# Fixing VectorE's order through the second attention branch of a decoder block, with its bias made in two halves

## The chip, the cores and the metric

The kernel runs on one core of a Trainium2 chip. The metric is the time of one execution on the device, in microseconds (us). The engines are named as in the profile: PE is TensorE (PEld its weight loads), DVE is VectorE, ACT is ScalarE, POOL is GpSimd, SP is SyncE, which issues most DMAs.

## The reference

One layer of a decoder: 256 tokens, width 1024, float32. Two attention branches of eight heads of 64 share one input projection, their outputs are merged by a sigmoid gate, and a gated feed-forward network of width 2816 follows. With 256 tokens the block-sparse first branch is plain causal attention. The second branch adds a "forgetting" bias to its scores, and this is where the change lies:

```python
def forgetting_attention(q, k, v, log_f):
    c = jnp.cumsum(log_f, axis=-1)
    ...
        s = jnp.einsum('bhcd,bhsd->bhcs', qi, k, ...) * scale
        s = s + ci[..., None] - c[:, :, None, :]
        s = jnp.where(pos[None, :] <= qp[:, None], s, NEG_INF)
        p = jax.nn.softmax(s, axis=-1).astype(v.dtype)
...
proj = jnp.einsum('bsd,de->bse', rms_norm(x, attn_norm_g[l]), w_in[l])
qa, ka, va, qb, kb, vb, f_logit, g_logit = jnp.split(proj, bounds, axis=-1)
o_a = moba_attention(qa, ka, va)          # after head norms and rope
o_b = forgetting_attention(qb, kb, vb, log_sigmoid(f_logit + b_forget))
merged = gates[:, :, 0] * (o_a @ w_branch_moba) + gates[:, :, 1] * (o_b @ w_branch_fox)
x = x + merged @ w_out
u, g = jnp.split(rms_norm(x, ffn_norm_g) @ w_ffn_up, 2, axis=-1)
x = x + (silu(causal_depthwise_conv(g)) * u) @ w_ffn_down
```

## The kernel before

Every float32 matrix product is made of three products of a reduced type: an operand is split into an upper part (`whi`, `xh`, `oh`) and a lower rest (`wlo`, `xl`, `ol`), and upper times upper, lower times upper and upper times lower are added in PSUM. Weights come from memory in chunks of 128 x 2048 (`raw`, three buffers). Each chunk is split in two halves, "units" of 1024 columns: ScalarE copies the upper part (line 141) and VectorE subtracts it from the raw weight for the lower part (line 142). There are six buffers of `whi` and of `wlo`. A raw buffer is free for the next chunk's DMA when both of its units are split. `use` asks for a unit and starts splits some five units ahead.

The order of the chunks, and so of TensorE's work, is written in the list `chunks`. In the part that matters it is: gate 2 (`wg`, 2), the scores of the second branch, the V projection of the second branch (`qkv`, 3, in chunks 0 and 1, that is four units), gates 3, 4 and 5 (two units each), the transposes of both branches' probabilities (line 540), gate 6, the products with V (line 562), gate 7, then the output side and the feed-forward part.

TensorE runs in the order of the program. For the other engines a scheduler at compile time orders each queue, by priority (a block under `soon()` goes ahead of its place in the program) and by when it takes an instruction to be ready. `after(i, j)` adds an edge that keeps instruction i behind j in this order. On one engine that is only an order and costs no instruction; once compiled, each engine works off its queue strictly in turn.

VectorE's work in this part:

- `gate` (line 603) reads a gate's PSUM bank, scales it and writes it into `gates`.
- `forget_bias` (lines 451 to 465) makes the bias of all eight heads, 128 x 3072: per block of 128 keys a subtraction of the query's cumulated value (`cc`) from the keys' values (`cB`, which lies in the upper half of `gates` and is broadcast over the partitions by a DMA from GpSimd's queue, line 443), and for two of the three blocks an addition of the causal mask. These are five instructions of 128 x 1024.
- `scores` puts the four pairs of heads into six PSUM banks with small matmuls and has VectorE fill the unused corners with zeros (ten fills, line 489).
- `softmax` (line 508) reads each pair's scores from PSUM in four instructions, adds the bias, keeps the row's extreme in `nm` and writes to SBUF. ScalarE then takes four exponentials per pair (line 512), with sums in `l`, and VectorE the reciprocals `r` (line 516).
- `scale` multiplies by `r`: for pairs 0 and 1 of the second branch on GpSimd (line 524), for pairs 2 and 3 on VectorE (line 528, four instructions a pair); the first branch is scaled by ScalarE (line 530).

PSUM has eight banks, given out in turn. The six of the second branch's scores, the two of the V projection and then the bank of gate 3 follow each other. Gate 3's bank is therefore the first of the score banks again: pair 0's scores of the first head and part of pair 1's lie in it, so it is free when those are read.

Of the kernel before, what the change touches and what calls it, by code (L numbers as in the profile page):

```python
# [12 lines left out]
ALU = mybir.AluOpType  # L13
# [4 lines left out]
P = 128  # L18
# [4 lines left out]
HD = 64  # L23
NH = 8
# [20 lines left out]
def decoder_block(ctx, tc, a, out):  # L45
    nc = tc.nc
# [50 lines left out]
    moved = []  # L97
    sent_last = []
    first_lo = []
    state = {"next": 0, "raw": None, "lag": 0, "hi": None, "lo": None}  # L100

    def after(i, j):
# [2 lines left out]
    def load(upto):  # L105
        while state["next"] <= min(upto, len(units) - 1):
            c, h = units[state["next"]]
            if c[0] == "head":
                k = c[1]
                if k < 2:  # L110
                    raw = gates[:, 4 * k:4 * k + 4].rearrange("p a b t -> p (a b t)")
                    for s0, s1 in ((0, HX + W4), (HX + W4, HEADW)):
                        loads[c] = nc.sync.dma_start(raw[:, s0:s1], a["head"][k][:, s0:s1])
                    x, g, raw = raw[:, 0:S], raw[:, S:S + 1], raw[:, HX:HEADW]
                    nc.gpsimd.tensor_copy(xT[:, k], x)
                else:
                    if k % 2 == 0:
                        state["raw"] = T([P, 2048], "raw", RB)
                    raw = state["raw"][:, k % 2 * 1024:(k % 2 + 1) * 1024]
                    x, g = xT[:, k], g1[:, k:k + 1]  # L120
                    nc.sync.dma_start(x, a["head"][k][:, 0:S])
                    loads[c] = nc.sync.dma_start(raw, a["head"][k][:, HX:HEADW])
                xlo = split_x(k, x, g)
                at, n = 44, 2 if k < 2 else 1
            else:
                at, n = 44 if c[0] == "qkv" else 0, 1
                if h == 0:
                    src = a[c[0]]
                    for j in c[1:]:
                        src = src[j]  # L130
                    state["raw"] = T([P, 2048], "raw", RB)
                    loads[c] = nc.sync.dma_start(state["raw"], src)
                    if c in (("qkv", 0, 1), ("wg", 2)):
                        after(loads[c], sent_last[c == ("wg", 2)])
                raw = state["raw"][:, h * 1024:(h + 1) * 1024]
            hi = T([P, 1088], "whi", HB, F32R)[:, at:at + 1024]
            lo = T([P, 1088], "wlo", HB, F32R)[:, at:at + 1024]
            w = 1024 // n
            for j in range(n):
                s = slice(j * w, (j + 1) * w)  # L140
                i = nc.scalar.activation(hi[:, s], raw[:, s], AF.Copy)  # L141
                d = nc.vector.tensor_tensor(lo[:, s], raw[:, s], hi[:, s].bitcast(F32), op=ALU.subtract)  # L142
                if (c, h) == (("qkv", 1, 1), 0):
                    after(i, rs_done[0])
                    after(d, rs_done[1])
                if (c, h) == (("qkv", 1, 0), 0):
                    first_lo.append(d)
                if (c, h) == (("qkv", 0, 1), 0):
                    after(i, moved[0])
                if (c, h) in ((("qkv", 2, 1), 1), (("wg", 0), 1)):  # L150
                    after(d, state["qn"])
                if (c, h) == (("wg", 1), 0):
                    after(i, state["exp"])
                if (c, h) == (("qkv", 0, 0), 0):
                    state["v_lo"] = d
                if (c, h) == (("wg", 1), 1):
                    state["turn"] = d
                if (c, h) == (("qkv", 3, 0), 1):
                    state["v1_lo"] = d
                if (c, h) == (("qkv", 3, 1), 0):  # L160
                    after(i, state["v_out"])
                if c[0] == "head" and j == 0:
                    after(d, xlo)
                for this, last in ((i, state["hi"]), (d, state["lo"])):
                    if last is not None:
                        after(this, last)
            if c[0] == "head":
                square_x(k, x, i)
            split[c, h] = (hi, lo)
            state["last"] = i, d  # L170
            state["next"] += 1
# [276 lines left out]
            step = 6 if i < 2 else 2  # L448
            nc.gpsimd.tensor_copy(cc[32 * i:32 * (i + 1)], turned[:, i:i + step + 1:step, 0:NH])

    def forget_bias(done):

        bias = fg["bias"] = T([P, 3072], "bias").rearrange("p (n c) -> p n c", n=NH)
        for j, (kb, t) in enumerate([(0, 0), (1, 1), (0, 1)]):
            dst = bias[:, :, j * P:(j + 1) * P]
            src = fg["cB"][:, :, kb * P:(kb + 1) * P]
            if kb:
                d4, src = (v.rearrange("p n (h c) -> p n h c", h=2) for v in (dst, src))
                i = nc.vector.tensor_tensor(d4, src[:, :, ::-1], cc[:, t, :, None, None].to_broadcast([P, NH, 2, HD]), op=ALU.subtract)
                after(i, done)  # L460
            else:
                i = nc.vector.tensor_tensor(dst, src, cc[:, t, :, None].to_broadcast([P, NH, P]), op=ALU.subtract)
                after(i, done)
            if j != 2:
                nc.vector.tensor_tensor(dst, dst, mask3[:, None, j * P:(j + 1) * P].to_broadcast([P, NH, P]), op=ALU.add)


    probs = {}
    homes = []
    last_exp = []  # L470

    def scores(br, read):
        sps = [banks() for _ in range(3)]
        at = [((0, 0), (0, P)), ((0, 3 * P), (1, 0)), ((2, 0), (1, S)), ((2, P), (2, S))]
        def piece(n, t, j):
            b, o = at[n][t]
            return sps[b][j][:, o:o + (t + 1) * P]
        for n, pair in enumerate(range(4)):
            for t in range(NT):
                for c, q in enumerate(QUARTERS[t]):  # L480
                    seen = slice(0, (q + 1) * HD) if t == 0 else slice((3 - q) * HD, S)
                    keys = slice(seen.start + (1 - t) * P, seen.stop + (1 - t) * P)
                    for j, r in enumerate(halves):
                        nc.tensor.matmul(piece(n, t, j)[halves[c], seen], qTs[br][r, pair, q * HD:(q + 1) * HD], kTs[br][r, pair, keys], start=True, stop=True)
        for b, c, o in ((0, 0, slice(64, 512, 384)), (0, 1, slice(128, 129, 1)), (1, 1, slice(0, 512, 256)), (2, 0, slice(64, 256, 128)), (2, 1, slice(256, 257, 1))):
            for j in range(2):
                starts = range(o.start, o.stop, o.step)
                u = sps[b][j][halves[c]].rearrange("p (g c) -> p g c", c=HD)[:, o.start // HD:starts[-1] // HD + 1:max(1, o.step // HD)]
                after(nc.vector.memset(u, 0.0), read)
        return [[[piece(n, t, j) for t in range(NT)] for j in range(2)] for n in range(4)]  # L490

    def softmax(br, pair, sps, done, exp_behind=None):
# [11 lines left out]
        for j in range(2):  # L504
            h = 2 * pair + j
            sp = sps[j]
            for i, c in enumerate((slice(0, 128), slice(128, 384))):
                first = nc.vector.tensor_tensor_reduce(s[:, j, c], sp[i], mask3[:, c] if br == 0 else fg["bias"][:, h, c],
                                               scale=1.0, scalar=3e38, op0=ALU.add, op1=ALU.min, accum_out=nm[:, j, i:i + 1])
                after(first, done)  # L510
            for i, c in enumerate((slice(0, 128), slice(128, 384))):
                last_exp[:] = [nc.scalar.activation(s[:, j, c], s[:, j, c], AF.Exp, scale=-1.0, bias=nm[:, j, i:i + 1], accum_out=l[:, j, i:i + 1])]  # L512
                if exp_behind is not None:
                    after(last_exp[0], exp_behind)
# [5 lines left out]
    def scale(br, pair, last=None):  # L520
        s, r = probs[br, pair]
        for i, c in enumerate((slice(0, 128), slice(128, 384))):
# [2 lines left out]
                continue  # L525
            for j in range(2):
                if br:
                    nc.vector.tensor_scalar_mul(s[:, j, c], s[:, j, c], r[:, j, i:i + 1])
                else:
                    after(nc.scalar.activation(s[:, j, c], s[:, j, c], AF.Copy, scale=r[:, j, i:i + 1]), last)  # L530
        probs[br, pair] = s
# [130 lines left out]
    project(2, pv, 1)  # L662
    finish_v(pv, 0, last_exp[0])
    read = gate(2)
    after(read, state["v1_lo"])
    with soon():
        forget_bias(state["last"][1])
    for pair in range(4):
        scale(0, pair, state["last"][0])
    with soon():  # L670
        for pair, sp in enumerate(scores(1, read)):
            softmax(1, pair, sp, read)
            scale(1, pair)
# [1 line left out]
    project(5, pv, 0)  # L675
    project(5, pv, 1)
    finish_v(pv, 1)
    gate(3)
    gate(4)
    gate(5, hold=True)  # L680
    with soon():
# [212 lines left out]
```

## Time and profile before

| | us |
|---|---|
| median of 3 runs (361.47 to 362.01) | 361.87 |
| the profiled execution | 361.6 |
| its span, first to last instruction | 359.8 |
| PE busy | 352.3 (98%) |
| DVE busy | 278.4 (77%) |
| ACT busy | 221.7 (62%) |
| POOL busy | 44.6 (12%) |

A row of the order in time gives the start in us from the span's start, the duration, engine, line and operation, the tile written and those read, and how many instructions are merged in the row; in brackets stands idle time before it and what ended that. A row of waits gives waiter, what it waited for, total us, times and the longest. A row of the stretches gives the stretch, its length, and for each engine (PE, PEld, DVE, ACT, POOL) busy time and instructions, then TensorE's granted clock, the DMA share and GB/s. Ends of matmuls are modelled, so starts are used.

### The profile page before, as it was taken

The page shows a single profiled execution, that of the slowest core. Times are in us where ns is not written, and L with a number is a line of the kernel's source. Part 1 is how long each engine was busy: PE and PEld are TensorE (multiplying, and loading weights), DVE is VectorE, ACT ScalarE, POOL GpSimd, SP SyncE. Part 2 cuts the span into 40 slices and gives each one's busy share as a digit, 9 for nine tenths or more (in the row PEclk, how much of TensorE's full clock was granted, in tenths as well). Part 3 has the DMA queues.
Part 4 walks back from the last instruction along what each step waited for, and adds up shares of the span by engine and source line. Part 5 has one row for each costly group of instructions (what it writes and reads, how often), then busy time and mean ns, then how long its engine had stood idle before and what let it go on. Part 6 is the DMA issues. An engine that isn't in the chain of part 4 may idle for free.

```text
span 359.8 us, 7495 instructions
## 1 busy us (share of the span) xinstructions
PE 352.3 (98%) x3053; PEld 335.1 (93%) x3053; DVE 278.4 (77%) x476; ACT 221.7 (62%) x378; POOL 44.6 (12%) x69
## 2 busy tenths in 40 slices
PE   9999999999889999999999999999999999999995
PEld 5888899898789999999999999999999999999995
DVE  5899999979997668975969777768676866768643
ACT  5859644799984996645877554555464555546420
POOL 3432724230230000000530000000000000000000
PEclk9999999999999999999999999999999999999999
DMA  7987376958047454565464564564564564554003
GB/s 272 402 321 254 119 227 200 351 198 304 13 165 298 145 210 134 219 233 197 157 213 169 205 233 148 203 229 147 211 222 154 210 219 148 220 196 156 3 0 118
DMA packets 13475, 70.39 MB, mean 196 GB/s; under 512 B 2200, under 2 KB 3360, under 8 KB 6016
## 3 DMA queue, kind: packets, MB, share of 16 engines
q1 hardware_dynamic: 12624, 67.93, 52.9%
q0 software_dynamic: 672, 1.98, 1.7%
q8 instruction: 24, 0.39, 0.4%
q14 instruction: 11, 0.09, 0.1%
q10 hardware_dynamic: 144, 0.00, 0.0%
HBM read 66.75 MB, written 1.06 MB: 188 GB/s over the span
## 4 chain that ended last, share of the span: by engine, by line
PE 90%; ACT 5%; DVE 4%; issue 1%; DVEq 0%
PE bank L593 14%; PE bank L595 14%; PE bank L594 14%; PE bank L317 9%; PE bank L303 6%; PE bank L807 6%; PE bank L806 6%; PE bank L808 6%; PE bank L732 2%; PE bank L706 2%; DVE wlo L142 2%; PE bank L731 2%; PE bank L730 2%; PE bank L705 2%; PE bank L704 2%; ACT s L512 2%
## 5 line engine op out<-in xcount | busy, mean ns | idle before, releaser
L142 DVE TENSOR_TENSOR wlo<-raw,whi 128x1024 fp32r<-128x1024 f32 x120 | 146.8, 1230 | 47.3 <-ACT whi L141 47.0
L141 ACT ACTIVATE whi<-raw 128x1024 fp32r<-128x1024 f32 x120 | 125.2, 1059 | 62.7 <-PE bank L594 37.1
L595 PE MATMUL bank<-oh,wlo 128*128 128x256 f32 x352 | 96.8, 275 | 0.0
L593 PE MATMUL bank<-oh,whi 128*128 128x256 f32 x352 | 96.8, 275 | 0.0
L594 PE MATMUL bank<-ol,whi 128*128 128x256 f32 x352 | 96.8, 275 | 0.0
L593 PEld LDWEIGHTS bank<-oh,whi 128*128 128x128 f32 x352 | 66.1, 188 | 0.0
L595 PEld LDWEIGHTS bank<-oh,wlo 128*128 128x128 f32 x352 | 66.1, 188 | 0.0
L594 PEld LDWEIGHTS bank<-ol,whi 128*128 128x128 f32 x352 | 66.1, 188 | 0.0
L593 PE MATMUL bank<-xh,whi 128*128 128x256 f32 x128 | 35.7, 279 | 1.5 <-ACT ol L512 1.5
L595 PE MATMUL bank<-xh,wlo 128*128 128x256 f32 x128 | 35.4, 276 | 1.3 <-DVE wlo L142 1.3
L594 PE MATMUL bank<-xl,whi 128*128 128x256 f32 x128 | 35.3, 276 | 0.0
L593 PEld LDWEIGHTS bank<-xh,whi 128*128 128x128 f32 x128 | 24.0, 188 | 2.6 <-ACT ol L512 1.9
L595 PEld LDWEIGHTS bank<-xh,wlo 128*128 128x128 f32 x128 | 24.0, 188 | 1.5 <-DVE wlo L142 1.5
L594 PEld LDWEIGHTS bank<-xl,whi 128*128 128x128 f32 x128 | 24.0, 188 | 0.1
L317 PE MATMUL bank<-whi,xh 128*128 128x512 f32 x64 | 21.2, 391 | 0.1
L317 PE MATMUL bank<-wlo,xh 128*128 128x512 f32 x64 | 21.0, 388 | 0.0
L317 PE MATMUL bank<-whi,xl 128*128 128x512 f32 x64 | 21.0, 388 | 0.0
L773 DVE TENSOR_TENSOR sq<-bank,rs 128x512 f32<-128x512 f32 x22 | 15.1, 692 | 6.6 <-PE bank L595 6.5
L704 PE MATMUL bank<-oh,whi 128*128 128x256 f32 x64 | 17.6, 275 | 0.0
L705 PE MATMUL bank<-ol,whi 128*128 128x256 f32 x64 | 17.6, 275 | 0.0
L706 PE MATMUL bank<-oh,wlo 128*128 128x256 f32 x64 | 17.6, 275 | 0.0
L730 PE MATMUL bank<-xh,whi 128*128 128x256 f32 x64 | 17.6, 275 | 0.0
(197 smaller groups left out, 762.3 us busy)
## 6 DMA issues: line engine op xcount, KB each, us to landing
raw<-in_wu SPq DMA_DIRECT2D x22, 1024.0 KB, 4.8
raw<-in_wd SPq DMA_DIRECT2D x11, 1024.0 KB, 4.8
raw<-in_qkv SPq DMA_DIRECT2D x8, 1024.0 KB, 5.6
raw<-in_wg SPq DMA_DIRECT2D x8, 1024.0 KB, 4.9
raw<-in_wb SPq DMA_DIRECT2D x4, 1024.0 KB, 5.0
raw<-in_wo SPq DMA_DIRECT2D x4, 1024.0 KB, 4.9
raw<-in_head SPq DMA_DIRECT2D x6, 512.0 KB, 6.6
gates<-cd POOLq DMA_DIRECT2D x1, 1024.0 KB, 8.0
```

The lines of the kernel that those rows point to most:

```text
L141: i = nc.scalar.activation(hi[:, s], raw[:, s], AF.Copy)
L142: d = nc.vector.tensor_tensor(lo[:, s], raw[:, s], hi[:, s].bitcast(F32), op=ALU.subtract)
L303: nc.tensor.matmul(pt[t], lhs[:, k, t * P:(t + 1) * P], rhs, start=(k == 0 and i == 0), stop=(k == KT - 1 and i == 2))
L317: nc.tensor.matmul(pt[t], lhs[:, k, t * P:(t + 1) * P], rhs[:, c], start=(k == 0 and i == 0), stop=(k == KT - 1 and i == 2))
L593: nc.tensor.matmul(o, wh[:, w], mh[:, k], start=(k == 0 and i == 0), stop=False)
L594: nc.tensor.matmul(o, wh[:, w], ml[:, k], start=False, stop=False)
L595: nc.tensor.matmul(o, wl[:, w], mh[:, k], start=False, stop=(k == KT - 1 and i == 1))
L704: nc.tensor.matmul(o, wh[:, w], oh[:, 4 * br + k], start=(k == 0), stop=False)
L705: nc.tensor.matmul(o, wh[:, w], ol[:, 4 * br + k], start=False, stop=False)
L706: nc.tensor.matmul(o, wl[:, w], oh[:, 4 * br + k], start=False, stop=(k == 3))
L730: nc.tensor.matmul(o, wh[:, w], mh[:, k], start=(k == 0 and i == 0), stop=False)
L806: nc.tensor.matmul(o, wh[:, w], ah, start=(p == 0 and h == 0 and c == 0), stop=False)
```

## The change

`forget_bias` is split in two calls, one for heads 0 to 3 and one for heads 4 to 7, each with five instructions of 128 x 512. Each lower-half split is kept by its unit (`los`), and the fills, score reads and late scalings are gathered in lists. After gate 3 a list `order` sets out VectorE's instructions from gate 2's read on, and each group is put behind all of the group before it: gate 2's read, the ten fills, the first half of the bias, the V projection's third split, pair 0's score reads, its fourth split, pair 1's reads, both splits of gate 3's weights, the second half of the bias, pair 2's reads, the first split of gate 4, pair 3's reads, the read of gate 3, the second split of gate 4, the first of gate 5, the scalings of pair 2, the second split of gate 5, the scalings of pair 3. Reciprocals are not in the list, nor is any other engine's work.

```diff
-    def forget_bias(done):
-
-        bias = fg["bias"] = T([P, 3072], "bias").rearrange("p (n c) -> p n c", n=NH)
+    def forget_bias(part):
+        if part == 0:
+            fg["bias"] = T([P, 3072], "bias").rearrange("p (n c) -> p n c", n=NH)
+        n0, n = 4 * part, 4
+        bias = fg["bias"][:, n0:n0 + n]
+        ops = []
         for j, (kb, t) in enumerate([(0, 0), (1, 1), (0, 1)]):
             dst = bias[:, :, j * P:(j + 1) * P]
-            src = fg["cB"][:, :, kb * P:(kb + 1) * P]
+            src = fg["cB"][:, n0:n0 + n, kb * P:(kb + 1) * P]
...
+                ops.append(nc.vector.tensor_tensor(dst, src, cc[:, t, n0:n0 + n, None].to_broadcast([P, n, P]), op=ALU.subtract))
             if j != 2:
-                nc.vector.tensor_tensor(dst, dst, mask3[:, None, j * P:(j + 1) * P].to_broadcast([P, NH, P]), op=ALU.add)
+                ops.append(nc.vector.tensor_tensor(dst, dst, mask3[:, None, j * P:(j + 1) * P].to_broadcast([P, n, P]), op=ALU.add))
+        return ops
...
-                after(nc.vector.memset(u, 0.0), read)
+                fills.append(nc.vector.memset(u, 0.0))
+                after(fills[-1], read)
...
+                reads.setdefault((br, pair), []).append(first)
...
-                    nc.vector.tensor_scalar_mul(s[:, j, c], s[:, j, c], r[:, j, i:i + 1])
+                    scaled_late.append(nc.vector.tensor_scalar_mul(s[:, j, c], s[:, j, c], r[:, j, i:i + 1]))
...
     with soon():
-        forget_bias(state["last"][1])
+        bias = forget_bias(0), forget_bias(1)
...
-    gate(3)
+    third = gate(3)
+    v1, wg3, wg4, wg5 = ("qkv", 3, 1), ("wg", 3), ("wg", 4), ("wg", 5)
+    order = [[read], fills, bias[0], [los[v1, 0]], reads[1, 0], [los[v1, 1]], reads[1, 1], [los[wg3, 0]], [los[wg3, 1]],
+             bias[1], reads[1, 2], [los[wg4, 0]], reads[1, 3], [third], [los[wg4, 1]], [los[wg5, 0]],
+             scaled_late[:4], [los[wg5, 1]], scaled_late[4:]]
+    for first, then in zip(order, order[1:]):
+        for i in then:
+            for j in first:
+                after(i, j)
```

Before, the whole bias was kept behind the last split issued by then; that edge goes.

More of the change, by code (lines that the diff above doesn't have):

```diff
@@ L99, in decoder_block @@
     first_lo = []
+    los = {}
+    scaled_late = []
     state = {"next": 0, "raw": None, "lag": 0, "hi": None, "lo": None}
@@ L157, in load @@
                     state["turn"] = d
-                if (c, h) == (("qkv", 3, 0), 1):
-                    state["v1_lo"] = d
+                los[c, h] = d
                 if (c, h) == (("qkv", 3, 1), 0):
@@ L449, in forget_chain @@
             nc.gpsimd.tensor_copy(cc[32 * i:32 * (i + 1)], turned[:, i:i + step + 1:step, 0:NH])
-    def forget_bias(done):
-        bias = fg["bias"] = T([P, 3072], "bias").rearrange("p (n c) -> p n c", n=NH)
+    def forget_bias(part):
[4 more added lines that the diff above has]
+        ops = []
         for j, (kb, t) in enumerate([(0, 0), (1, 1), (0, 1)]):
             dst = bias[:, :, j * P:(j + 1) * P]
-            src = fg["cB"][:, :, kb * P:(kb + 1) * P]
+            src = fg["cB"][:, n0:n0 + n, kb * P:(kb + 1) * P]
             if kb:
                 d4, src = (v.rearrange("p n (h c) -> p n h c", h=2) for v in (dst, src))
-                i = nc.vector.tensor_tensor(d4, src[:, :, ::-1], cc[:, t, :, None, None].to_broadcast([P, NH, 2, HD]), op=ALU.subtract)
-                after(i, done)
-            else:
-                i = nc.vector.tensor_tensor(dst, src, cc[:, t, :, None].to_broadcast([P, NH, P]), op=ALU.subtract)
-                after(i, done)
+                ops.append(nc.vector.tensor_tensor(d4, src[:, :, ::-1], cc[:, t, n0:n0 + n, None, None].to_broadcast([P, n, 2, HD]), op=ALU.subtract))
+            else:
+                ops.append(nc.vector.tensor_tensor(dst, src, cc[:, t, n0:n0 + n, None].to_broadcast([P, n, P]), op=ALU.subtract))
             if j != 2:
-                nc.vector.tensor_tensor(dst, dst, mask3[:, None, j * P:(j + 1) * P].to_broadcast([P, NH, P]), op=ALU.add)
+                ops.append(nc.vector.tensor_tensor(dst, dst, mask3[:, None, j * P:(j + 1) * P].to_broadcast([P, n, P]), op=ALU.add))
+        return ops
     probs = {}
@@ L470, in decoder_block @@
     last_exp = []
+    fills = []
+    reads = {}
     def scores(br, read):
@@ L664, in decoder_block @@
     read = gate(2)
-    after(read, state["v1_lo"])
+    after(read, los[("qkv", 3, 0), 1])
     with soon():
-        forget_bias(state["last"][1])
+        bias = forget_bias(0), forget_bias(1)
     for pair in range(4):
@@ L670, in decoder_block @@
     with soon():
+        fills.clear()
         for pair, sp in enumerate(scores(1, read)):
```

## The prediction

> **What bounds the kernel now.** I read the page first for the busiest engine, then the table of stretches and the waits of TensorE, and then the instructions in order of time on TensorE, VectorE, ScalarE and GpSimd between 82 and 113 us.
>
> ```profile
> span 359.8 us, 7495 instructions
> PE 352.3 (98%) x3053; PEld 335.1 (93%) x3053; DVE 278.4 (77%) x476; ACT 221.7 (62%) x378; POOL 44.6 (12%) x69
> ...
> PE bank L593 <- ACT ol L512: 1.5, 1, 1.5
> PE bank L595 <- DVE wlo L142: 1.3, 1, 1.3
> ...
> 105.20:113.30 8.10, 8.10 (x70) 7.98 (x70) 7.23 (x11) 2.71 (x3) 0.00 (x0) 1.00 0.81 288
> 113.30:133.00 19.70, 19.70 (x357) 19.37 (x357) 11.22 (x14) 18.92 (x35) 0.29 (x1) 1.00 0.53 204
> 140.00:180.00 40.00, 40.00 (x355) 40.00 (x355) 33.96 (x50) 23.36 (x35) 5.14 (x6) 1.00 0.52 187
> ```
>
> TensorE (PE) is busy 98% of the span at granted clock 1.00 (first figure behind the stretches' busy times), and has two waits of size, both inside the code that the diff orders. Once past 105.2 us it has no idle time in the stretches shown. So the kernel ends as early as TensorE passes that point, if nothing later falls behind. These rows place the two waits:
>
> ```profile
> 88.93 0.61 PE L317 MATMUL bank<-wlo,xh 128*128 128x512 f32 x2
> 91.65 0.61 PE L317 MATMUL bank<-wlo,xh 128*128 128x512 f32 x2
> 93.01 0.61 PE L317 MATMUL bank<-wlo,xh 128*128 128x512 f32 x2
> 95.16 0.36 PE L593 MATMUL bank<-xh,whi 128*128 128x256 f32 x1 [1.53 <-ACT ol L512]
> 103.55 0.28 PE L594 MATMUL bank<-xl,whi 128*128 128x256 f32 x1
> 105.14 0.38 PE L595 MATMUL bank<-xh,wlo 128*128 128x256 f32 x1 [1.32 <-DVE wlo L142]
> ```
>
> The V projection's matmuls are 0.227 us apart (12 from 88.93 to 91.65), those of a gate 0.115 (73 from 95.16 to 103.55). The last projection matmul starts at 93.01 + 0.227, so gate 3 could start at 93.46; its bank is the one from which pairs 0 and 1 of the scores are read (bank rotation in the code). Without waits, the lower halves of wg3 and wg4 (wlo, each used from a half's third matmul on) would be due at 93.7, 96.5, 99.2 and 102.0. The last was used at 105.14: TensorE is 3.2 us late there, and no gain can be larger. What it waits for is VectorE's queue:
>
> ```profile
> 81.62 0.68 DVE L603 TENSOR_TENSOR gates<-bank,rsB 128x512 f32<-128x512 f32 x1
> 82.39 0.58 DVE L489 MEMSET bank<- 64x128 f32 x4
> 83.53 2.36 DVE L142 TENSOR_TENSOR wlo<-raw,whi 128x1024 fp32r<-128x1024 f32 x2 [0.56 <-ACT whi L141]
> 85.81 1.22 DVE L462 TENSOR_TENSOR bias<-gates,cc 128x1024 f32<-128x1024 f32 x1
> 86.95 1.22 DVE L459 TENSOR_TENSOR bias<-gates,cc 128x1024 f32<-128x1024 f32 x1
> 91.60 0.97 DVE L489 MEMSET bank<- 64x128 f32 x6
> 92.48 0.27 DVE L508 CUSTOM_DVE_ANT_0 ol<-bank,bias 128x128 f32<-128x128 f32 x1
> 94.73 0.28 DVE L508 CUSTOM_DVE_ANT_0 ol<-bank,bias 128x128 f32<-128x128 f32 x1
> 95.84 0.07 DVE L508 DVE_READ_ACCUMULATOR2_ANT nm<- 128x1 f32 x1
> 96.52 0.18 DVE L516 RECIPROCAL r<-l 128x4 f32<-128x4 f32 x1 [0.61 <-ACT ol L512]
> 96.61 1.20 DVE L142 TENSOR_TENSOR wlo<-raw,whi 128x1024 fp32r<-128x1024 f32 x1
> 98.90 1.47 DVE L142 TENSOR_TENSOR wlo<-raw,whi 128x1024 fp32r<-128x1024 f32 x1
> 103.27 0.68 DVE L603 TENSOR_TENSOR gates<-bank,rsB 128x512 f32<-128x512 f32 x1
> 103.88 2.34 DVE L142 TENSOR_TENSOR wlo<-raw,whi 128x1024 fp32r<-128x1024 f32 x2
> ...
> 76.62 0.56 POOL L443 DMA_DIRECT2D gates<-cd  x1 [0.52 <-POOL cc L449]
> gates<-cd POOLq DMA_DIRECT2D x1, 1024.0 KB, 8.0
> ```
>
> The whole bias (five instructions from 85.81, next work 91.60) stands ahead of every score read. Pair 1's first read starts only at 94.73, and 95.16 follows it; the waits' list names ScalarE there, whose work ended in the same tenth, and below it makes no difference. The split of wg4's second half starts at 103.88 and releases TensorE 1.26 us later.
>
> **The change part by part.** Only VectorE's instructions are ordered; the order itself adds none. Five bias instructions of 1024 columns become ten of 512, of which five come early and five behind wg3's splits. A 1024-column instruction takes the queue 1.14 (85.81 to 86.95), a 512-column one 0.61 (L603, 103.27 to 103.88), so a half costs 3.05 and the whole 6.1 in place of 5.7. (No row shows this operation at 512 columns: half of 1.14 would be 0.57, the full 0.68 of L603 the upper end, so the early half and the late one together may be 0.4 shorter or 0.7 longer; I take L603's step, the nearest.) A split takes 1.14, a pair's four score reads 1.11 (94.73 to 95.84), ten fills 0.58 + 0.88 = 1.46. The sum follows the written order:
>
> - gate 2's read is where it was. Ten fills, six of them now ahead of the bias instead of behind it, run from 82.39, where four start today, to 83.85; their banks' scores are in, since the projection behind them on TensorE runs by then. Bias needs the broadcast of the cumulated gates, which lands at 76.62 + 8.0 = 84.62; before, two splits covered that, now nothing does, and VectorE idles 0.8. First bias half 84.65 to 87.70.
> - the V projection's third unit: 87.70 to 88.84. The product that needs it starts at 88.93 and the release takes 1.26 from the start, 88.96: just in time. Pair 0's reads to 89.95. Fourth unit to 91.09, released 91.21, needed 91.65. Pair 1's reads to 92.20; gate 3's bank is free near 91.5, before 93.46. The first wait goes.
> - wg3's two splits to 94.48, released 93.46 and 94.60 against 93.7 and 96.5. Second bias half to 97.53, pair 2's reads to 98.64, wg4's first split to 99.78 (released 99.90, due 99.2: a new wait of 0.7), pair 3's reads to 100.89, gate 3's read to 101.50. wg4's second split starts at 101.50, not 103.88: 2.38 earlier.
>
> From this come off the reciprocals, which the order leaves free: 0.09 each (96.52 to 96.61) for up to three, 0.27. That leaves 2.1 before what GpSimd takes. GpSimd scales pairs 0 and 1 while VectorE runs this queue, and the two get in each other's way:
>
> ```profile
> 98.25 1.03 POOL L524 TENSOR_TENSOR ol<-ol,r 128x512 f32<-128x512 f32 x1
> 99.25 1.59 POOL L524 TENSOR_TENSOR ol<-ol,r 128x256 f32<-128x256 f32 x1
> 100.57 1.89 DVE L528 TENSOR_SCALAR qn<-qn,r 128x128 f32<-128x128 f32 x4
> 107.34 0.99 DVE L528 TENSOR_SCALAR qn<-qn,r 128x128 f32<-128x128 f32 x4
> 174.88 1.68 POOL L746 TENSOR_TENSOR sqs<-sqs,sq 128x256 f32<-128x256 f32 x1
> 175.88 1.85 DVE L739 SCALAR_TENSOR_TENSOR ol<-xT,sm,oh 128x256 fp32r<-128x256 f32 x2
> 179.39 0.87 DVE L739 SCALAR_TENSOR_TENSOR ol<-xT,sm,oh 128x256 fp32r<-128x256 f32 x2
> ```
>
> A split that started under GpSimd's scaling took 1.47 in place of 1.22 (the time of the bias rows of its size), and four scalings 1.89 in place of 0.99: together 1.15 in before's queue ahead of 103.88. At 175.88 two VectorE instructions with both tensors in SBUF took 0.98 longer beside GpSimd's adds. In the new order the same four GpSimd instructions meet mostly splits and bias, which read two SBUF tensors. Lower end 0 (they fall on score reads, whose scores lie in PSUM). Upper end, all four block for their length: the long form 1.03, the short one 1.59 less VectorE's hold until 100.37 (98.90 + 1.47), 0.47: twice 1.50 is 3.0. I take 1.0, nearest to what the same four cost before.
>
> [...]
>
> Sum: 2.38 - 0.27 - 1.0 = 1.1 gained. The profiled execution took 361.6 (span 359.8 and 1.8 around it); the median shown, 361.87, is 0.27 above. From the median: 360.8.
>
> If ScalarE and not the bank released 95.16, and does so at the same time again, TensorE would be 1.7 late there; the last split, with the tolls, leaves it 2.1 late anyway, so the sum stands.
>
> **Costed at nothing.** The scalings of pairs 2 and 3 move back behind wg5's splits: 101.5 + three splits and two sets of four (0.92 each) + the tolls left is about 107.5, needed by the transposes near 113; cover 5 us, and without it up to 1.8. Queue of loads: wg5's buffer is freed by the V projection's fourth split, now 91.1 and not 85.8, so its load (4.9 to landing, the row below) is there at 96; gate 5 needs its split near 105.
>
> ```profile
> raw<-in_wg SPq DMA_DIRECT2D x8, 1024.0 KB, 4.9
> 89.89 3.89 ACT L141 ACTIVATE whi<-raw 128x1024 fp32r<-128x1024 f32 x4
> 96.39 0.39 ACT L512 ACTIVATE ol<-ol,nm 128x128 f32<-128x128 f32 x1
> 98.14 0.39 ACT L512 ACTIVATE qn<-qn,nm 128x128 f32<-128x128 f32 x1
> ```
>
> wg6 and wg7 free theirs earlier than now. GpSimd's queue keeps its order. ScalarE's order is not fixed by the diff, and that is the open part.
>
> **The rivals.**
>
> 1. Slower: ScalarE takes the exponentials first. Before, it makes four upper halves at 89.89, then the exponentials. With reads two to three us earlier, eight exponentials (1.75 for four, 96.39 to 98.14) can stand ahead of wg3's upper half: 89.89 + 3.5 + 0.97 = 94.36. VectorE, now bound to its order, stands at wg3's first split from 92.3 until 94.4, 2.1 us, with bias and the reads behind it. Then 2.1 - 2.1 - 1.0 = a loss of 1.0: 362.9. It decides once that wait and GpSimd's toll pass 2.1 together. For it: ScalarE ran 1.75 of exponentials without a split between at 96.39. Against: four upper halves went first before.
> 2. No change that shows: GpSimd's toll is near its upper end: 3.0, or 2.4 if a fifth of it falls on the 2.2 us of score reads among some 10 us; then between 0.3 and 0.9 is lost, 362.5. For it: 175.88. Against: 98.90, where VectorE lost 0.25 to an instruction of 1.03. [...]
> 3. No change that shows: reciprocals stand early in VectorE's queue and wait for their exponentials. Before, one such wait is 0.61 (96.52); two of them take the 1.1 to nothing: 361.9.
>
> **How the numbers follow.** Forecast as summed 0.53 (toll 0 to 1.5: gain 0.6 to 2.1, so 359.8 to 361.3); rival 1 0.19; rival 2 0.15; rival 3 or something late behind 113 us 0.13. Faster than 0.2% (0.72 us, about what can be told from no change): nearly all of the first, 0.50. Slower: rival 1 and the far half of rival 2, 0.22. Within: 0.28. The range for 8 in 10 reaches from the gain without a toll, 359.7, to rival 1 with its spread, 363.0.
>
> **What would show it.** Gate 3 starts near 93.5 without the 1.5 wait; ten 512-column bias instructions of about 0.69; wg4's second split starts near 102.8; a short wait at gate 4's first half; no TensorE idle time behind it. It would be wrong if VectorE shows a wait on ScalarE's upper half at wg3, if splits or bias instructions are stretched by over 1.5 us together, or if TensorE gets a new wait at the transposes.

## The result and the profile after

The changed kernel takes 364.20 us (median of 6 runs, 363.08 to 365.07) against 361.83 for the kernel before on the same chip: ratio 1.0065, 95% interval 1.0043 to 1.0088. It is slower by 0.65%, where 360.8 was predicted. The profiled execution took 363.35, 1.75 more than the one of before (361.6).

The page's lines and TensorE's waits after:

```profile
span 361.6 us, 7500 instructions
PE 353.0 (98%) x3053; PEld 335.0 (93%) x3053; DVE 279.0 (77%) x481; ACT 221.4 (61%) x378; POOL 43.8 (12%) x69
...
PE bank L603 <- DVE wlo L144: 3.8, 2, 2.1
```

The two waits of before (1.5 and 1.3) have become two of 3.8 together, both for a lower half of weights. TensorE in order of time places them; the third row is the first of the transposes, and the last, of the kernel before, shows where they started there:

```profile
96.10 0.39 PE L603 MATMUL bank<-xh,wlo 128*128 128x256 f32 x1 [1.75 <-DVE wlo L144]
103.95 0.39 PE L603 MATMUL bank<-xh,wlo 128*128 128x256 f32 x1 [2.09 <-DVE wlo L144]
115.04 1.15 PE L548 MATMUL bank<-cst,s 64*128 64x64 f32 x30
...
113.31 1.72 PE L540 MATMUL bank<-cst,s 64*128 64x64 f32 x48
```

The transposes come 1.73 later, the execution is 1.75 longer: nothing is lost behind the transposes. Of the 1.73, 0.35 was there when VectorE read gate 2's bank (81.97 against 81.62), ahead of the changed code; such shifts show in the other executions too (in the traces of this document that read starts between 81.52 and 82.38). The other 1.4 lies between gate 2 and the transposes. VectorE's queue in order of time shows where:

```profile
81.97 0.68 DVE L611 TENSOR_TENSOR gates<-bank,rsB 128x512 f32<-128x512 f32 x1
82.74 1.52 DVE L495 MEMSET bank<- 64x128 f32 x10
84.99 0.69 DVE L465 TENSOR_TENSOR bias<-gates,cc 128x512 f32<-128x512 f32 x1 [0.72 <-DMA gates<-cd]
...
90.25 0.08 DVE L515 DVE_READ_ACCUMULATOR2_ANT nm<- 128x1 f32 x1
...
91.94 0.08 DVE L515 DVE_READ_ACCUMULATOR2_ANT nm<- 128x1 f32 x1
94.03 0.18 DVE L524 RECIPROCAL r<-l 128x4 f32<-128x4 f32 x1 [2.01 <-ACT ol L520]
94.12 0.26 DVE L515 CUSTOM_DVE_ANT_0 ol<-bank,bias 128x128 f32<-128x128 f32 x1
...
94.66 3.37 DVE L144 TENSOR_TENSOR wlo<-raw,whi 128x1024 fp32r<-128x1024 f32 x2
...
102.14 1.76 DVE L144 TENSOR_TENSOR wlo<-raw,whi 128x1024 fp32r<-128x1024 f32 x1
...
105.60 1.21 DVE L144 TENSOR_TENSOR wlo<-raw,whi 128x1024 fp32r<-128x1024 f32 x1
```

Read the row at 94.03. Pair 0's reciprocal works for 0.18 us, and VectorE had stood 2.01 for it, between the second and the third score read of pair 1. The list `order` doesn't name the reciprocals, so the scheduler put this one where it took it to be ready. ScalarE's order says why it wasn't:

```profile
90.25 1.99 ACT L143 ACTIVATE whi<-raw 128x1024 fp32r<-128x1024 f32 x2
92.15 0.38 ACT L520 ACTIVATE ol<-ol,nm 128x128 f32<-128x128 f32 x1
...
93.81 0.18 ACT L520 ACTIVATION_READ_ACCUMULATOR ol<-ol,nm 128x1 f32 x1
```

Two upper halves stand ahead of pair 0's exponentials, which end at 93.99, and VectorE goes on at 94.03. GpSimd is released at the same time, and its scalings (pair 0, then pair 1, a short and a long instruction each) run beside splits. The last row is the first of the two splits at 94.66 by itself:

```profile
94.36 0.61 POOL L532 TENSOR_TENSOR ol<-ol,r 128x256 f32<-128x256 f32 x1 [17.00 <-DVE r L524]
94.94 2.01 POOL L532 TENSOR_TENSOR ol<-ol,r 128x512 f32<-128x512 f32 x1
101.21 0.61 POOL L532 TENSOR_TENSOR ol<-ol,r 128x256 f32<-128x256 f32 x1 [4.26 <-DVE r L524]
101.78 1.04 POOL L532 TENSOR_TENSOR ol<-ol,r 128x512 f32<-128x512 f32 x1
...
94.66 1.39 DVE L144 TENSOR_TENSOR wlo<-raw,whi 128x1024 fp32r<-128x1024 f32 x1
```

The two splits at 94.66 took 3.37; the two at 83.53 of before, undisturbed, took 2.36. The one at 102.14 took 1.76 in place of 1.22. So GpSimd took 1.01 + 0.54 = 1.55 from this queue. Each of the three splits ends 1.08 after the GpSimd instruction that it met: 96.05 after 94.97, 98.03 after 96.95, 103.90 after 102.82. The three equal distances fit a split that waits for that instruction to end. The long one at 94.94, in its turn, took 2.01 in place of 1.04 beside the first split.

### The profile page after: what moved, and what is told of

It is laid out like the page before. It is cut to its first block, busy times and chain, and to the rows that moved or that the text cites. A ratio compares the mean times of both kernels' runs of the same rounds, so it can differ in the third digit from the quotient of the medians.

```text
span 361.6 us, 7500 instructions
## 1 busy us (share of the span) xinstructions
PE 353.0 (98%) x3053; PEld 335.0 (93%) x3053; DVE 279.0 (77%) x481; ACT 221.4 (61%) x378; POOL 43.8 (12%) x69
## 4 chain that ended last, share of the span: by engine, by line
PE 87%; ACT 7%; DVE 4%; issue 1%; DVEq 0%
PE bank L601 14%; PE bank L603 14%; PE bank L602 14%; PE bank L304 6%; PE bank L318 6%; PE bank L823 6%; PE bank L825 6%; PE bank L824 6%; DVE wlo L144 3%; PE bank L748 2%; PE bank L722 2%; PE bank L749 2%; PE bank L747 2%; PE bank L723 2%; PE bank L721 2%; ACT whi L143 2%
```

## The experiments

Lines are those of each kernel's own profile; a few lines added to the code move its line numbers by one or two. A ratio is to the kernel before, timed on the same chip.

**1. Pair 0's reciprocal alone put behind gate 3's splits** (`recips[1]` lists the second branch's reciprocals in the order of the pairs).

```diff
+    after(recips[1][0], los[wg3, 1])
```

> The changed kernel with one edge more: pair 0's reciprocal behind wg3's second split. The queue then has the reciprocals of pairs 0 and 1 together behind the second half of the bias. Theory 1 (in the changed kernel VectorE stands 2.0 us at pair 0's reciprocal, which waits for ScalarE's exponentials with pair 1's last reads and wg3's splits queued behind it, and GpSimd's scaling stretches three splits by 1.6 together): the 2.0 goes whole, GpSimd's toll moves behind the bias to wg4's first split and stays 0.5 to 1.0; about 2.5 to 3 us under the changed kernel, 361.0 to 361.6. Theory 2 (the early half of the bias, its wait for the broadcast and the half-size instructions are what costs): no change, 363 to 365. Theory 3 (GpSimd's toll alone): at most 1.6 less, 362.5.

Measured: 363.05 (362.16 to 365.34), ratio 1.0038 [1.0021, 1.0054]. The first theory's 361.0 to 361.6 is missed. VectorE's queue:

```profile
92.78 2.36 DVE L144 TENSOR_TENSOR wlo<-raw,whi 128x1024 fp32r<-128x1024 f32 x2
...
99.30 1.79 DVE L144 TENSOR_TENSOR wlo<-raw,whi 128x1024 fp32r<-128x1024 f32 x1
...
103.85 0.18 DVE L525 RECIPROCAL r<-l 128x4 f32<-128x4 f32 x1 [2.21 <-ACT qn L521]
```

Gate 3's splits run at 92.78 without a wait or a stretch. But pair 2's reciprocal now stands among pair 3's reads and holds the queue for 2.21, and GpSimd stretches gate 4's split (1.79 in place of 1.22). The same fault moved eight microseconds on: one free instruction was bound, another took its place.

**2. All four reciprocals behind the first split of gate 5.**

```diff
+    for i in recips[1]:
+        after(i, los[wg5, 0])
```

> The changed kernel with all four reciprocals of the second branch behind wg5's first split, so GpSimd's scaling starts only there as well. Theory 1: both the wait of 2.0 and the toll of 1.6 are gone from the queue ahead of wg4's second split; the written order runs at its own length, the split starts near 101.8 instead of 105.6, and the kernel takes 359.3 to 360.0, under the kernel before. Theory 2: 363 to 365, at the changed kernel's time. Theory 3: 362.5. If something behind 113 us falls late (scalings, transposes), a new wait of TensorE shows there.

Measured: 361.64 (361.23 to 362.74), ratio 0.9991 [0.9982, 1.0000]. The loss is gone; the expected gain isn't there. VectorE's queue first:

```profile
84.65 0.69 DVE L465 TENSOR_TENSOR bias<-gates,cc 128x512 f32<-128x512 f32 x1 [0.61 <-DMA gates<-cd]
...
101.41 2.35 DVE L144 TENSOR_TENSOR wlo<-raw,whi 128x1024 fp32r<-128x1024 f32 x2
...
104.99 0.18 DVE L525 RECIPROCAL r<-l 128x4 f32<-128x4 f32 x1 [1.02 <-ACT qn L521]
105.09 2.54 DVE L538 TENSOR_SCALAR qn<-qn,r 128x128 f32<-128x128 f32 x4
...
110.20 3.49 DVE L144 TENSOR_TENSOR wlo<-raw,whi 128x1024 fp32r<-128x1024 f32 x3
113.60 0.68 DVE L613 TENSOR_TENSOR gates<-bank,rsB 128x512 f32<-128x512 f32 x1
```

With the reciprocals out of the way, gate 4's second split starts at 101.41. TensorE in order of time:

```profile
99.83 0.39 PE L605 MATMUL bank<-xh,wlo 128*128 128x256 f32 x1 [0.39 <-DVE wlo L144]
108.81 0.39 PE L605 MATMUL bank<-xh,wlo 128*128 128x256 f32 x1 [0.38 <-DVE wlo L144]
111.56 1.71 PE L550 MATMUL bank<-cst,s 64*128 64x64 f32 x48
...
114.34 1.06 PE L550 MATMUL bank<-cst,ol 64*128 64x64 f32 x23 [1.01 <-DVE gates L613]
```

The transposes start 1.75 earlier than before (111.56 against 113.31), and then wait 1.01 for a read of gate 5's bank that stands behind three splits of 3.49. The gain is earned at gates 3 to 5 and handed back at the transposes, since VectorE's queue is late there: scalings stretched from 0.99 to 2.54 beside GpSimd, a reciprocal's wait of 1.02, and splits that nothing needs yet ahead of a read that TensorE waits for.

**3. GpSimd's scalings of pairs 0 and 1 left out** (part of the computation is missing, so this measures only what that work costs the other engines).

```diff
-                nc.gpsimd.tensor_tensor(s[:, :, c], s[:, :, c], r[:, :, i:i + 1].to_broadcast([P, 2, c.stop - c.start]), op=ALU.mult)
```

> The changed kernel without GpSimd's four scalings: pairs 0 and 1 of the second branch are left unscaled. VectorE's order stays, with the reciprocal's wait of 2.0. Theory 1: the three stretched splits (3.37 for two, 1.76 for one) go back to 2.36 and 1.22, 1.5 us less: 362.0 to 362.8. Theory 2: no change, 363 to 365. Theory 3: the whole difference to the kernel before goes, 361.8 or less.

Measured: 362.44, ratio 1.0013 [1.0005, 1.0022]. VectorE's queue:

```profile
93.93 0.18 DVE L524 RECIPROCAL r<-l 128x4 f32<-128x4 f32 x1 [1.34 <-ACT ol L520]
...
94.56 2.36 DVE L144 TENSOR_TENSOR wlo<-raw,whi 128x1024 fp32r<-128x1024 f32 x2
...
101.01 1.22 DVE L144 TENSOR_TENSOR wlo<-raw,whi 128x1024 fp32r<-128x1024 f32 x1
...
103.35 0.18 DVE L524 RECIPROCAL r<-l 128x4 f32<-128x4 f32 x1 [0.57 <-ACT qn L520]
```

All three stretched splits are back at 2.36 and 1.22, so the stretch was GpSimd's work; and the kernel is still not faster than before, because the reciprocals' waits stay. In this run VectorE also waits longer for the broadcast (1.39, against 0.54 to 0.79 in the other profiles where it waits for it), which hides part of what GpSimd gave back; 362.44 is therefore no clean price.

**4. The bias in halves, no order written out.** `done`, new in `forget_bias`, is the last split issued by then, as in the kernel before.

```diff
+        for i in ops:
+            after(i, done)
...
-    for first, then in zip(order, order[1:]):
-        for i in then:
-            for j in first:
-                after(i, j)
```

> The bias in two halves, but both kept behind the last split issued as the bias is in the kernel before, and without the written order. VectorE's order is that of the kernel before but for ten bias instructions in place of five. Theory 1: the halves cost 0.3 to 0.4 of VectorE's time, both waits of TensorE stay: 361.8 to 362.3. Theory 2: most of the change's loss is here already, 363 or more.

Measured: 362.00, ratio 1.0007 [0.9999, 1.0016]: no difference that shows. The loss belongs to the order. TensorE's waits there:

```profile
95.60 0.35 PE L603 MATMUL bank<-xh,whi 128*128 128x256 f32 x1 [1.87 <-DVE nm L517]
105.44 0.39 PE L605 MATMUL bank<-xh,wlo 128*128 128x256 f32 x1 [1.17 <-DVE wlo L144]
```

Gate 3 waits for a score read of VectorE (`nm`): the bank, not ScalarE's exponentials that the list of before named. The times of the rows agree: gate 3 starts 0.43 after the start of pair 1's first score read, here (95.17 and 95.60) as before (94.73 and 95.16) and in experiment 7 (94.62 and 95.05). Before, ScalarE's last exponential ahead of it ended at 95.04, only 0.12 earlier, so the list could name it.

**5. The tail ordered too.** Experiment 2, with the reciprocals behind gate 5's second split, both splits of gate 5 ahead of the scalings, and gate 5's read ahead of gate 6's second split:

```diff
+    for i in recips[1]:
+        after(i, los[wg5, 1])
...
-             bias[1], reads[1, 2], [los[wg4, 0]], reads[1, 3], [third], [los[wg4, 1]], [los[wg5, 0]],
-             scaled_late[:4], [los[wg5, 1]], scaled_late[4:]]
+             bias[1], reads[1, 2], [los[wg4, 0]], reads[1, 3], [third], [los[wg4, 1]], [los[wg5, 0]], [los[wg5, 1]],
+             scaled_late[:4], scaled_late[4:]]
...
-    gate(5, hold=True)
+    fifth = gate(5, hold=True)
+    after(los[("wg", 6), 1], fifth)
```

> The run with late reciprocals, with its tail ordered too: both splits of wg5 ahead of the reciprocals and the scalings, and the read of gate 5 ahead of wg6's second split. Theory 1 (in the run with late reciprocals TensorE reached the transposes 1.75 us earlier than in the kernel before and gave 1.5 back there, since the read that frees gate 5's bank stood behind three splits): the wait of 0.4 at gate 5 and that of 1.0 at the transposes go, gate 6 starts 1.8 us earlier, 359.7 to 360.2. Rival (the transposes are bound by something else that only shows when they come early, such as the banks that ScalarE empties or the scaled probabilities): the transposes wait for another releaser and the time stays at 361.3 to 361.9.

Measured: 360.64, ratio 0.9966 [0.9946, 0.9987], faster, but short of the expected. The wait for gate 5's read is gone, and one of 0.97 for a copy of transposes has come, behind two splits of gate 6 (TensorE, order in time):

```profile
110.90 1.71 PE L550 MATMUL bank<-cst,s 64*128 64x64 f32 x48
...
114.63 0.71 PE L550 MATMUL bank<-cst,qn 64*128 64x64 f32 x15 [0.97 <-DVE pT L556]
```

So the gain handed back at the transposes was a matter of VectorE's order, and was only half mended.

**6. As 5, and the V projection's third split ahead of the first half of the bias**, where VectorE idled for the broadcast:

```diff
-    order = [[read], fills, bias[0], [los[v1, 0]], reads[1, 0], [los[v1, 1]], reads[1, 1], [los[wg3, 0]], [los[wg3, 1]],
+    order = [[read], fills, [los[v1, 0]], bias[0], reads[1, 0], [los[v1, 1]], reads[1, 1], [los[wg3, 0]], [los[wg3, 1]],
```

> The same, with the V projection's third split moved ahead of the first half of the bias, where VectorE idles 0.6 for the broadcast. Theory 1: the queue ends some 0.5 earlier, the wait of 0.4 at gate 4's first half goes, 359.2 to 359.8. If the broadcast's landing is no part of the path: no difference to the kernel with the tail alone.

Measured: 359.61, ratio 0.9945 [0.9932, 0.9957]. The idle time before the bias is filled with a split, and the waits at gates 3 to 5 are gone; the copy's wait stays.

```profile
84.43 1.21 DVE L144 TENSOR_TENSOR wlo<-raw,whi 128x1024 fp32r<-128x1024 f32 x1
85.56 0.67 DVE L465 TENSOR_TENSOR bias<-gates,cc 128x512 f32<-128x512 f32 x1
```

**7. The kernel before, with only its reciprocals moved** behind gate 4's second split:

```diff
+    for i in recips[1]:
+        after(i, los[("wg", 4), 1])
```

> The kernel before with one rule more: the second branch's four reciprocals behind wg4's second split, so that GpSimd's scaling, and the wait of 0.6 at pair 0's reciprocal, leave the queue ahead of it. Nothing else of the change. Theory 1 (reciprocals and GpSimd's toll cost before's queue some 2 us too): wg4's second split starts near 101 in place of 103.88, the wait of 1.3 at gate 4 goes, the wait of 1.5 at gate 3 stays: 360.4 to 360.9. Rival (the order and the halves are what shortens the queue, the reciprocals matter only in the changed kernel): 361.8 to 362.2.

Measured: 361.03, ratio 0.9978 [0.9969, 0.9987], just above the range of theory 1. Gate 4's second split starts at 100.22 in place of 103.88 and gate 4's wait is gone; the 1.5 at gate 3 stays. Without any written order, four binding edges gain a fifth of a per cent: in before's queue too, the place of the reciprocals made the second wait. But their own wait is the smaller part of the 3.66. The rows of the two queues give 0.61 for it, 0.27 for the work of three reciprocals and 0.25 for the split that GpSimd had stretched; 1.81 is pair 2's scalings, which follow their reciprocal behind the split, 0.61 is gate 3's read, which the scheduler now puts behind it as well, and 0.10 was there at gate 2's read.

```profile
100.22 1.21 DVE L143 TENSOR_TENSOR wlo<-raw,whi 128x1024 fp32r<-128x1024 f32 x1
101.36 0.68 DVE L607 TENSOR_TENSOR gates<-bank,rsB 128x512 f32<-128x512 f32 x1
...
104.89 3.08 DVE L532 TENSOR_SCALAR qn<-qn,r 128x128 f32<-128x128 f32 x8
```

**8. The changed kernel once more, unedited**, for its spread of 2 us (the kernel before lay within 0.54 in the first comparison; in the one made with this run, two of its 17 executions were outside that, at 362.87 and 364.32):

> The changed kernel once more, for its spread: six runs lay between 363.1 and 365.1, those of the kernel before between 361.5 and 362.0. If the spread comes from how GpSimd's and VectorE's instructions fall on each other, this profile shows the stretched splits at other places or of other lengths than 3.37 for two and 1.76 for one, by as much as its time differs from 363.35; if from the broadcast's landing, the idle time before the bias differs instead (0.7 so far).

Measured: 364.22 (362.91 to 365.17), ratio 1.0065 [1.0039, 1.0090]; the profiled execution took 365.13. Neither expected cause is there: the broadcast's idle time is 0.79 (0.72 in the first profile), the stretched splits take 3.37 and 1.77 (3.37 and 1.76), and TensorE's waits are 1.68 and 2.09 (1.75 and 2.09). The table of stretches, with the granted clock third from last, shows another:

```profile
95.00:97.00 2.00, 0.57 (x4) 0.57 (x5) 2.00 (x4) 2.00 (x10) 2.00 (x2) 1.00 0.50 205
...
101.00:104.00 3.00, 1.19 (x11) 0.99 (x9) 3.00 (x11) 3.00 (x11) 1.61 (x2) 1.00 0.57 240
...
105.50:109.00 3.50, 3.50 (x19) 3.50 (x19) 3.50 (x8) 1.89 (x6) 0.00 (x0) 0.52 0.21 42
```

The same stretch in the first profile of the changed kernel:

```profile
105.50:109.00 3.50, 3.50 (x32) 3.42 (x31) 3.50 (x9) 1.55 (x5) 0.00 (x0) 1.00 0.27 63
```

Soon after the two waits TensorE runs 3.5 us at a granted clock of 0.52 and gets 19 matmuls started where 32 start at 1.00. That is 13 matmuls of 0.115, 1.5 us, of the 1.78 by which the two executions differ; some 0.3 was there at gate 2's read (82.31 against 81.97).

**9. As 6, and the two copies of transposes ahead of gate 6's second split:**

```diff
-                    nc.vector.tensor_copy(dst[:, h, 8 * i:8 * i + 8], turned)
+                    copies.append(nc.vector.tensor_copy(dst[:, h, 8 * i:8 * i + 8], turned))
...
+    for i in copies:
+        after(los[("wg", 6), 1], i)
```

> The kernel of tail_and_v1 with one thing more: VectorE's two copies of the transposes out of the PSUM bank (the copies into pT) stand ahead of wg6's second split instead of behind it. In tail_and_v1 the transposes waited 1.02 us for such a copy, which had come behind splits. Theory (the wait is only a matter of VectorE's order): the wait of 1.0 at the transposes goes and the sixth gate starts about 0.8 to 1.0 earlier, so 358.6 to 359.0, provided that wg6's second split, now two copies (about 0.6 each) later, still comes before the sixth gate's products need it. Rival (something else is ready no sooner): ScalarE's copies of the other half of the transposes or wg6's second split hold TensorE in its place, and the time stays at 359.2 to 360.0, with one of these two named as the releaser.

Measured: 358.58 (358.20 to 358.92), ratio 0.9904 [0.9888, 0.9921]. This is the fastest version. TensorE's only listed wait is now one for its own sequencer (0.8, in every profile here), and the transposes run without a break:

```profile
PE bank L221 <- PEq L912: 0.8, 1, 0.8
```

```profile
110.40 1.71 PE L551 MATMUL bank<-cst,s 64*128 64x64 f32 x48
111.94 0.91 PE L551 MATMUL bank<-cst,ol 64*128 64x64 f32 x24
112.69 0.91 PE L551 MATMUL bank<-cst,qn 64*128 64x64 f32 x24
```

They start 2.91 earlier than before, and its profiled execution is 2.93 shorter (358.67 against 361.6). How much of this the order of the diff is needed for isn't separated: the kernel before with its reciprocals bound and its tail ordered, but with the whole bias ahead of the reads, was not tried.

## Why the prediction was wrong

**The step that failed** is the term "the reciprocals, which the order leaves free: 0.09 each". They were priced by their work alone. The queue that they stand in is strictly in turn, so a free instruction costs what it waits for: 2.01 at one place. The prediction's third rival named this mechanism, but took its price from before (0.61 each) and had 361.9 come out. That price couldn't carry over. In before, pair 0's reads end before 94.73 and its reciprocal runs at 96.52, so 1.8 us lay between them for the exponentials; in the new order VectorE is done with pair 0's reads at 90.33 and with half of pair 1's at 92.02, while ScalarE begins the exponentials at 92.15 with 1.84 still to do. Moving the producer's input earlier moves nothing if the producer is busy.

**The sum, by its own terms.** Predicted start of gate 4's second split with all terms: 101.50 + 0.27 + 1.0 = 102.77. Measured 105.60. The difference of 2.83:

| term | predicted | measured |
|---|---|---|
| the order alone | 101.50 | 101.41 (experiment 2) |
| later start of the bias in this execution (gate 2's read was 0.35 later) | 0 | 0.34 (84.99 against 84.65) |
| reciprocals, work | 0.27 | 0.27 (0.09, from 94.03 to 94.12, three times) |
| reciprocals, wait | 0 | 2.01 |
| GpSimd's toll | 1.0 | 1.55 |
| sum | 102.77 | 105.58 |

The measured terms add up to within 0.02 of the start measured. So the reciprocals' wait is the step that failed, and GpSimd's toll is a second term that was taken too small. From the profiled execution of before, 361.6 - 1.1 + 2.83 gives 363.33, and 363.35 is what the profiled execution took. The median lies 0.85 above that. The fall of the clock (experiment 8) is the one source of such an excess that a profile showed, in one of two. The two executions of the changed kernel with a mean granted clock of 1.000 took 362.91 and 363.35, the eight with 0.993 to 0.995 took 363.08 to 365.17, three of them under 363.7. So every long one has the lower clock, but the lower clock does not always make a long one; what decides that stays open.

**What was right.** The length of the written order, to 0.09 in some 20 us: bias instructions of 0.68 to 0.69, the fills (1.52 against 1.46), the idle time for the broadcast (0.72 against 0.8), the reads and splits. The first wait was the bank's (the rows in experiment 4), and the order takes it away: in the changed kernel gate 3 waits for a lower half instead, and with the reciprocals bound it starts without a wait. The new wait at gate 4's first half, 0.7 by the sum, is 0.39 in experiment 2.

**Rival 1** (exponentials ahead of gate 3's upper halves) did not happen: ScalarE did the reverse, upper halves at 90.25 and exponentials at 92.15. The loss was larger than the 1.0 that this rival forecast (1.75 in the profiled executions, 2.4 by the medians), and came by the opposite order on the same engine.

**Rival 2.** The toll of 1.55 lies between the 1.0 taken and the 2.4 from which that rival starts, nearer to the first. The row at 94.31 within the stretch, a score read out of PSUM beside GpSimd's first instruction, keeps its 0.42. The same form took 0.42 at 89.35, with GpSimd idle. The three splits, which read two SBUF tensors, end 1.08 after the GpSimd instruction that each met.

```profile
94.31 0.42 DVE L515 CUSTOM_DVE_ANT_0 ol<-bank,bias 128x256 f32<-128x256 f32 x1
```

The prediction set the split at 98.90 of the kernel before against this rival, as it had lost only 0.25. It had met only the last 0.38 of its GpSimd instruction (98.25 to 99.28), and ended 1.09 after it, as the others did. The upper end of 3.0 was missed for another reason: it let all four instructions hold VectorE for their length, but the short ones at 94.36 and 101.21 fell wholly or by half on score reads, and the long one at 101.78 ran beside reads until the split at 102.14. What the prediction lacked was which instruction lies beside which. Experiment 2's scalings, which read one SBUF tensor and a scalar for each row, were stretched as well (2.54 against 0.99).

**Costed at nothing: the tail, "cover 5 us".** That was reckoned for the scalings alone. Experiment 2 shows that the cover was gone for what stands around them: gate 5's read and the copies of the transposes, behind splits and stretched scalings, took back 1.0 of the 1.75 won there, and some of the rest went into the transposes that followed. In the changed kernel itself this cost nothing, as TensorE was later still.

**The bound.** "No gain can be larger" than 3.2: experiment 9 reaches it, 0.96% or 3.4 us, by its interval 2.9 to 4.1; its profiled execution gained 2.93, although its gate 2 was read later than before: near 82.05 against 81.62, an estimate from experiment 6's 82.22 and the 0.17 by which its queue runs ahead of that one (gate 4's first split at 98.14 against 98.31).

## What to carry to other kernels

An order written out for an engine binds only what it names, and an engine that works its queue in turn is held by the smallest instruction left free (here 2.01 us by a reciprocal of 0.18): name every instruction that waits for another engine, or place it behind work that is long enough. Price an unnamed instruction by its producer's place in the producer's own queue, not by its duration or by a wait in the old order. When a queue is pulled forward, look for the next read that TensorE waits for behind work that is not yet due; here binding the reciprocals (experiment 2) and three further changes of the order (experiments 5, 6 and 9) turned a loss of 0.65% into a gain of 0.96%.

## What the runs showed of the hardware that was not expected

Two waits of TensorE of 1.68 and 2.09, 8 us apart, were followed by 3.5 us at a granted clock of 0.52 in one execution (about 1.5 us lost), and two of 1.75 and 2.09 by none in another. So 3.8 us of stalls can be followed by a further loss of 1.5, and not in every execution. That the waits bring the clock down was not tested, but the mean granted clocks on record go with them. A mean of 0.995 or less shows in 8 of 10 executions of the changed kernel, in 3 of 12 of experiment 1 (waits of 1.05 and 2.17) and in 4 of 11 of experiment 4 (1.87 and 1.17); it shows in none of 59 of the kernel before (1.53 and 1.32) and in none of the other variants, whose waits in the profiles reach 1.52. In experiment 4 it cost nothing that shows: those four took 361.88 to 362.22, the other seven 361.78 to 362.46.
